# Start of a one-layer decoder kernel: small weights in three loads, K's first quarter moved up, zero products, a set order for TensorE

## The chip, the cores and the metric

The kernel runs on one core of one Trainium2 chip. The metric is device time in microseconds (us) of one execution, the median over repeated runs. Engines are named as the profile does: PE (TensorE) does the matrix products, PEld is its weight load, ACT is ScalarE, DVE is VectorE, POOL is GpSimd, SP is SyncE, which here issues nearly all loads.

## What is computed

One layer of a hybrid decoder, batch 1, 512 positions, model width 1024, all float32. Cut to what matters here:

```python
def reference(x, norm_mix_g, w_in, conv_a_w, gdn_conv_w, gdn_A_log, gdn_dt_bias, gdn_norm_g,
              w_a_out, w_b_out, w_o, norm_ffn_g, w_up, ffn_conv_w, w_down, norm_final_g):
    h = rmsnorm(x, norm_mix_g)
    bg, cg, xv, q, k, v, z, a, b, ga, gb = split(h @ w_in)      # a and b are 8 wide, the others 1024
    y_a = (bg * causal_dwconv(cg * xv, conv_a_w)) @ w_a_out
    y_b = gdn_branch(q, k, v, z, a, b, gdn_conv_w, gdn_A_log, gdn_dt_bias, gdn_norm_g) @ w_b_out
    x = x + (sigmoid(ga) * y_a + sigmoid(gb) * y_b) @ w_o
    h = rmsnorm(x, norm_ffn_g)
    x = x + conv_ffn(h, w_up, ffn_conv_w, w_down)               # D_FF = 2816
    return rmsnorm(x, norm_final_g)
```

The change touches only the beginning: the first `rmsnorm`, the turned activations, and the first products with `w_in` (those of `k`, and of `a` and `b`).

## The kernel before

**Products in two parts.** Every large product is made of three products of a one-pass type (fp32r): a float32 operand is split into a rounded part (`wh`, `hT[0]`) and the rest (`wl`, `hT[1]`), and high times high, high times low and low times high are added up in PSUM. The rounded part is made by ACT, the rest by DVE. Weights come as *blocks* of 1 MB, 256 output columns each; a block has four quarters (256 KB), and each quarter is split by one ACT copy and one DVE subtraction (`Block.part`, L135 to L141). A list of *jobs* (block, use) is worked through by `run_jobs`; the split of the next block is fed in while the products of the current one are issued. Block 0 is K, columns 0 to 255; block 1 is Q.

**The beginning, stage by stage.** `x` comes in four tiles `xt` of 128 positions (512 KB; the first two in halves). For a tile t: `norm_x(t)` squares and sums (ACT, L480), turns the sum into a factor (DVE L485 and L482, then a power on POOL, L486); `scale_x(t)` multiplies (DVE, L491); `turn_x(t)` transposes the tile on PE in eight pieces of 128 columns k = 0 to 7 (L496). Tiles 0 and 1 are the first half of the positions, 2 and 3 the second. For each half and each k, `out_hi` makes `hT[0]` (ACT, L499) and `out_lo` makes `hT[1]` (DVE, L503), both with the norm's weight from the tile `wA`.

K's block is treated by hand: its quarters are loaded one by one (`load_k`, L379) and split by `round_k(q)` (ACT, L509) and `rest_k(q)` (DVE, L513). `k_tile(j, k)` issues three products for output column group j on the first half of the positions; `ab_tile(k)` two products for `a` and `b`. All of them go through `mm`, so the profile shows them at L108.

**Small weights.** Convolution weights, norm weights and the gates' biases are small. Before, `wr` (128 rows of 128, from three loads, L446 to L448) is transposed on PE and copied by DVE into `wA` (L535); `wr2` and `wr3` (three loads, L463 to L466) are transposed later and copied into `wF` (L573 to L575); `dtb` and `alg` are two loads that broadcast eight numbers to all partitions (L458, L460); `ab_raw` is one load (L450).

**What sets the order.** SP issues loads in program order. Between L528 and L571 the order on DVE, ACT and POOL is the written one (`manual_schedule`); the order on PE, and all that follows on every engine, is set at build time by a planner with its own estimates of when operands are ready. `tc.keep_in_program_order` pins an instruction behind the one that was written before it on its engine. A few products of zeros (`WARM`, L470) run on PE while the first loads are under way.

The order as it is written for the first half of the positions:

```python
            for ks in (lower, upper):
                for k in ks:
                    out_hi(0, bs, k)
                for k in ks:
                    out_lo(0, bs, k)
                    k_tile(0, k)
                    ab_tile(k)
                if ks is lower:
                    rest_k(1)
```

After it come `norm_x(2)`, `rest_k(3)`, `scale_x(2)`, `norm_x(3)`, `rest_k(2)`, `scale_x(3)`, then `k_tile(1, k)` for the lower four k, `turn_x(2)` and `turn_x(3)`, `k_tile(1, k)` for the upper four, and `out_hi` and `out_lo` of the second half.

## Time and profile before

| | |
|---|---|
| time, median of 3 runs | 966.83 us (965.64 to 966.93) |
| profiled execution | 966.41 us, of which the span is 964.7 us |
| busy in the span | PE 99%, DVE 77%, ACT 52%, POOL 16% |
| part that the change touches | from the start to about 31 us, where the products of block 1 begin |

The span is the time from the first to the last instruction of the program; the 1.7 us beside it lie outside the program. A row of the timeline gives start and duration in us, engine, line, operation, output and inputs, shapes and count, and in brackets how long the engine had stood idle before it and what ended that. A row of a table of stretches gives busy time and instructions of each engine, then the TensorE clock that was granted (1.00 is full), the busy share of the DMA engines and what they moved.

### The profile page before, as it was taken

What the parts mean: (1) busy time and instruction counts of PE and PEld (TensorE: products, weight loads), DVE (VectorE), ACT (ScalarE), POOL (GpSimd) and SP (SyncE); (2) the same over time, 40 slices, a digit from 0 to 9 for tenths busy, and PEclk for the clock granted to TensorE, in tenths of its full rate; (3) what the DMA queues carried; (4) which work ended last, traced back from release to release, by engine and by line L of the source; (5) the groups of instructions that cost most, each with busy time, mean ns of one, the idle gap of its engine ahead of it and who ended that gap; (6) DMA issues with size and microseconds to landing.
All of it is one profiled execution on the core that took longest, in us unless ns stands there. A gap on an engine that the chain in (4) does not pass through costs nothing.

```text
span 964.7 us, 16169 instructions
## 1 busy us (share of the span) xinstructions
PE 951.5 (99%) x6178; PEld 822.6 (85%) x6178; DVE 743.1 (77%) x1401; ACT 505.9 (52%) x1073; POOL 157.1 (16%) x251
## 2 busy tenths in 40 slices
PE   8999999999999999999999999999999999999996
PEld 6888887887878889999988888998889999888885
DVE  5968686796735957799863479999988888969775
ACT  6795656566444424444751235645645456546463
POOL 3330300202000202312232100223222210000000
PEclk9999999999999999999999999999999999999999
DMA  6443422213121456756878436594774783176332
GB/s 227 155 139 95 121 53 89 74 47 103 53 88 45 133 130 138 200 147 160 232 256 173 124 104 225 149 232 154 174 189 177 193 163 131 45 260 230 99 131 87
DMA packets 51630, 138.11 MB, mean 143 GB/s; under 512 B 21692, under 2 KB 22113, under 8 KB 42849
## 3 DMA queue, kind: packets, MB, share of 16 engines
q1 hardware_dynamic: 38864, 107.45, 32.5%
q0 software_dynamic: 12544, 29.37, 16.3%
q8 instruction: 48, 0.79, 0.3%
q14 instruction: 30, 0.24, 0.1%
q10 hardware_dynamic: 144, 0.26, 0.1%
HBM read 133.64 MB, written 32.78 MB: 173 GB/s over the span
## 4 chain that ended last, share of the span: by engine, by line
PE 91%; DVE 4%; ACT 1%; issue 1%; POOL 1%; POOLq 0%
PE ps L108 83%; PE ps L681 1%; PE ps L716 1%; DVE wl L141 1%; PE ps L890 1%; PE ps L910 1%; DVE h L1327 1%; PE ps L899 0%; DVE hn L1313 0%; PE ps L878 0%; PE ps L877 0%; PE ps L854 0%; PE ps L848 0%; POOL r L1311 0%; PE ps L792 0%
## 5 line engine op out<-in xcount | busy, mean ns | idle before, releaser
L108 PE MATMUL ps<-hT,wh 128*128 128x512 f32 (+1 forms) x1104 | 319.1, 368 | 1.6 <-ACT hT L499 1.5
L140 ACT CAST wh<-raw 128x512 fp32r<-128x512 f32 x350 | 203.0, 618 | 220.8 <-PE ps L108 142.5
L141 DVE TENSOR_TENSOR wl<-raw,wh 128x512 fp32r<-128x512 f32 x350 | 232.3, 689 | 58.5 <-ACT wh L140 57.5
L108 PEld LDWEIGHTS ps<-hT,wh 128*128 128x128 f32 x1104 | 197.4, 190 | 30.6 <-ACT hT L499 1.7
L108 PE MATMUL ps<-hT,wl 128*128 128x512 f32 (+1 forms) x552 | 195.4, 362 | 0.0
L108 PE MATMUL ps<-h,wh 128*128 128x512 f32 (+1 forms) x704 | 177.7, 341 | 0.4 <-DVE h L1327 0.4
L108 PEld LDWEIGHTS ps<-h,wh 128*128 128x128 f32 x704 | 122.3, 189 | 15.7 <-DVE h L1327 0.6
L108 PEld LDWEIGHTS ps<-hT,wl 128*128 128x128 f32 x552 | 104.6, 190 | 13.8
L108 PE MATMUL ps<-h,wl 128*128 128x512 f32 (+1 forms) x352 | 114.5, 341 | 0.0
L108 PE MATMUL ps<-wh,xs 128*128 128x512 f32 (+1 forms) x320 | 96.9, 384 | 0.0
L108 PEld LDWEIGHTS ps<-h,wl 128*128 128x128 f32 x352 | 66.6, 189 | 7.6
L108 PEld LDWEIGHTS ps<-wh,xs 128*128 128x128 f32 x320 | 59.6, 188 | 13.1
L223 POOL COPY gate<-raw 1x1 f32<-1x1 f32 x38 | 19.7, 518 | 272.9 <-DMA raw<-in_w_in_dram 119.7
L108 PE MATMUL ps<-wl,xs 128*128 128x512 f32 (+1 forms) x160 | 62.1, 388 | 0.0
L108 PE MATMUL ps<-ts,wh 128*128 128x256 f32 x320 | 56.2, 276 | 0.0
L338 DVE SCALAR_TENSOR_TENSOR cv<-ps,wA,cv 128x511 f32<-128x511 f32 (+2 forms) x72 | 53.2, 741 | 3.9 <-ACT cv L335 3.7
L140 ACT CAST wh<-raws 128x512 fp32r<-128x512 f32 x66 | 39.2, 618 | 26.9 <-PE ps L108 8.6
L141 DVE TENSOR_TENSOR wl<-raws,wh 128x512 fp32r<-128x512 f32 x66 | 42.9, 687 | 12.6 <-ACT wh L140 12.5
L161 DVE TENSOR_TENSOR raw<-raw 128x512 f32<-128x512 f32 x72 | 49.4, 686 | 1.4
L108 PEld LDWEIGHTS ps<-ts,wh 128*128 128x128 f32 x320 | 49.0, 188 | 0.0
L108 PE MATMUL ps<-us,wh 128*128 128x256 f32 x256 | 45.0, 276 | 0.0
L108 PE MATMUL ps<-yas,wh 128*128 128x512 f32 x128 | 40.3, 394 | 0.0
(316 smaller groups left out, 1546.2 us busy)
## 6 DMA issues: line engine op xcount, KB each, us to landing
raw<-in_w_in_dram SPq DMA_DIRECT2D x35, 1024.0 KB, 4.9
raw<-in_w_up_dram SPq DMA_DIRECT2D x22, 1024.0 KB, 5.0
dv<-in_w_down_dram POOLq DMA_DIRECT2D x50, 256.0 KB, 6.2
raws<-dv SPq DMA_DIRECT2D x8, 768.0 KB, 7.2
ov<-in_w_o_dram POOLq DMA_DIRECT2D x20, 256.0 KB, 5.1
raws<-in_w_down_dram SPq DMA_DIRECT2D x10, 512.0 KB, 5.0
raw<-in_w_a_out_dram SPq DMA_DIRECT2D x4, 1024.0 KB, 5.9
raw<-in_w_b_out_dram SPq DMA_DIRECT2D x4, 1024.0 KB, 8.0
```

Source lines behind the costliest of these rows:

```text
L108: pe.matmul(o, lhsT=a, rhs=b, start=start, stop=stop, skip_group_check=free)
L140: act.copy(out=wh, in_=src)
L141: dve.tensor_tensor(out=wl, in0=src, in1=wh.bitcast(F32), op=ALU.subtract)
L161: dve.tensor_tensor(out=r[q], in0=a, in1=b, op=op)
L223: tc.keep_in_program_order(pool.tensor_copy(out=gate[:, 0:1], in_=el[:, 0:1]))
L338: dve.scalar_tensor_tensor(out=dst[:, sh:], in0=src[:, :S - sh], scalar=wcol(j), in1=dst[:, sh:], op0=ALU.mult, op1=ALU.add)
L681: pe.transpose(out=o[:, n * P:(n + 1) * P], in_=src[:, n * P:(n + 1) * P], identity=ident)
L716: pe.matmul(o[:, i], lhsT=kqs[:, a, h, 0, sl], rhs=kqs[:, b, h, :, sl], start=a > 0, stop=a + b == 0)
L890: pe.matmul(o[:, 0:P], lhsT=TTf[:, f, :], rhs=rs[h], start=True, stop=True)
L910: pe.matmul(o[:, 0:P], lhsT=A[:, f, :], rhs=vns[h], start=True, stop=True)
L1327: dve.tensor_tensor(out=h2[1][:, 4 * g:4 * g + 4, t * P:(t + 1) * P], in0=ov, in1=hs.bitcast(F32), op=ALU.subtract)
```

## The change

- SP's loads: `load_k(0)` becomes the fifth load, right behind the four loads of `x`'s first half. The small weights come in three loads that the host has laid out: `small_mix` (128 x 128, straight into `wA`), `small_ab`, and `small_rest` (128 x 149: `wF`, `dtb` and `alg` side by side) as the last one. There are 13 loads instead of 19, and PE's three transposes of small weights and DVE's two copies of them are gone.
- PE gets three products of zeros of 128 columns behind `turn_x(0)` and two behind `turn_x(1)` (`busy`), in float32 like `WARM`.
- PE's order is now the written one too, up to L571. In it, four k at a time: for each k, high times high, high times low and the two products for `a` and `b`; then the four products with `wl`.
- DVE's `rest_k(0)` is moved from ahead of the first `out_lo` to behind the second one; `rest_k(1)` likewise to behind the second `out_lo` of the upper four.
- The split of block 1 (Q) is pinned in program order on ACT and DVE (`pinned`).

```diff
             wl = self.wl[name] = wp.tile([P, *self.quarter], F32R, tag="wl", bufs=WQ, name=nm("wl"))
-            act.copy(out=wh, in_=src)
-            dve.tensor_tensor(out=wl, in0=src, in1=wh.bitcast(F32), op=ALU.subtract)
+            ops = act.copy(out=wh, in_=src), dve.tensor_tensor(out=wl, in0=src, in1=wh.bitcast(F32), op=ALU.subtract)
+            if self.pinned:
+                for op in ops:
+                    tc.keep_in_program_order(op)
...
+    rest_w = const.tile([P, 133 + 2 * H], F32, name="rest_w")
+    wF = rest_w[:, 0:133]
+    dtb, alg = rest_w[:, 133:133 + H], rest_w[:, 133 + H:133 + 2 * H]
...
         load_x(0)
         load_x(1)
-        wr = st1.tile([P, P], F32, name="wr")
-        nc.sync.dma_start(out=wr[0:96], in_=gdn_conv_w.rearrange("o j (c p) -> (o j c) p", p=P))
-        nc.sync.dma_start(out=wr[96:120], in_=conv_a_w.rearrange("o j (c p) -> (o j c) p", p=P))
-        nc.sync.dma_start(out=wr[120:128], in_=norm_mix_g.rearrange("o (c p) -> (o c) p", p=P))
+        load_k(0)
+        nc.sync.dma_start(out=wA, in_=small_mix)
         ab_raw = st1.tile([P, ND, 16], F32, name="ab_raw")
-        nc.sync.dma_start(out=ab_raw, in_=w_ab)
-        load_k(0)
+        nc.sync.dma_start(out=ab_raw, in_=small_ab)
         load_k(1)
         load_x(2)
         load_x(3)
         load_k(3)
         load_k(2)
-        dtb = gs.tile([P, H], F32, name="dtb")
...
-        nc.sync.dma_start(out=wr3[66:67], in_=gdn_norm_g)
+        nc.sync.dma_start(out=rest_w, in_=small_rest)
...
+        def busy(n, cols):
+            for _ in range(n):
+                pe.matmul(po[:, 0:cols], lhsT=warm[:, 0:P], rhs=warm[:, 0:cols], start=True, stop=True)
+
+        busy(WARM, S)
...
+        def first_tiles(ks, q):
+            for i, k in enumerate(ks):
+                out_lo(0, bs, k)
+                if i == 1:
+                    rest_k(q)
+                for e in (0, 1):
+                    mm(o_k[0][:, 0:HS], piece(k_block.wh, 0, k), hT[e][:, k, 0:HS], k == 0 and e == 0, False)
+                ab_tile(k)
+            for k in ks:
+                mm(o_k[0][:, 0:HS], piece(k_block.wl, 0, k), hT[0][:, k, 0:HS], False, k == ND - 1)
...
-        with tc.manual_schedule(engines={mybir.EngineType.DVE, mybir.EngineType.Activation, mybir.EngineType.Pool}):
+        with tc.manual_schedule(engines={mybir.EngineType.DVE, mybir.EngineType.Activation, mybir.EngineType.Pool,
+                                         mybir.EngineType.PE}):
             norm_x(0)
             scale_x(0)
             turn_x(0, bs)
-            pe.transpose(out=po[:, 0:P], in_=wr, identity=ident)
+            busy(3, P)
             norm_x(1)
             round_k(0)
-            dve.tensor_copy(out=wA, in_=po[:, 0:P])
             scale_x(1)
             turn_x(1, bs)
+            busy(2, P)
             ab_split()
             round_k(1)
-            rest_k(0)
             o_ab, o_k = bank(), [bank(), bank()]
-            for ks in (lower, upper):
+            for q, ks in enumerate((lower, upper)):
                 for k in ks:
                     out_hi(0, bs, k)
-                for k in ks:
-                    out_lo(0, bs, k)
-                    k_tile(0, k)
-                    ab_tile(k)
-                if ks is lower:
-                    rest_k(1)
+                first_tiles(ks, q)
             norm_x(2)
...
-        po = bank()
-        pe.transpose(out=po[:, 0:66], in_=wr2, identity=ident[:66, :66])
-        pe.transpose(out=po[:, 66:133], in_=wr3, identity=ident[:67, :67])
-        dve.tensor_copy(out=wF, in_=po[:, 0:133])
...
     jobs.insert(14, jobs.pop(11))
+    jobs[1][0].pinned = True
```

## The prediction

> **What bounds the kernel now.** First the page: busy shares and the chain of work that ended last.

> ```profile
> PE 951.5 (99%) x6178; PEld 822.6 (85%) x6178; DVE 743.1 (77%) x1401; ACT 505.9 (52%) x1073; POOL 157.1 (16%) x251
> PE 91%; DVE 4%; ACT 1%; issue 1%; POOL 1%; POOLq 0%
> ```

> TensorE is the bound throughout, so a change at the start is worth what it brings forward the moment from which PE is never idle again. Second, PE's waits: in the first 45 us (four rows), and from there to the end (two rows); us, times, longest.

> ```profile
> PE ps L496 <- DVE xr L491: 1.6, 2, 1.2
> PE ps L470 <- DVE warm L431: 1.5, 1, 1.5
> PE ps L108 <- ACT hT L499: 1.5, 1, 1.5
> PE ps L108 <- DVE hT L503: 0.2, 1, 0.2
> ...
> PE ps L681 <- DVE vs L929: 0.5, 1, 0.5
> PE ps L108 <- DVE h L1327: 0.4, 1, 0.4
> ```

> All there is to gain from waits lies ahead of the products. Third, a table of stretches, cut where the granted clock (the fraction after POOL) changes.

> ```profile
> 4.86:8.27 3.41, 2.35 (x12) 1.16 (x10) 1.62 (x7) 1.52 (x6) 1.10 (x2) 1.00 0.76 245
> 8.27:11.69 3.42, 1.45 (x11) 1.21 (x11) 1.76 (x5) 2.12 (x6) 0.00 (x0) 1.00 0.86 304
> 11.69:15.10 3.41, 3.25 (x16) 2.74 (x15) 3.41 (x9) 3.41 (x9) 0.00 (x0) 0.50 0.70 230
> 15.10:19.28 4.18, 4.18 (x37) 4.10 (x36) 3.23 (x8) 1.84 (x4) 2.63 (x4) 1.00 0.70 237
> 30.00:40.00 10.00, 10.00 (x51) 8.46 (x51) 9.63 (x19) 7.15 (x12) 7.58 (x19) 1.00 0.48 188
> ```

> The clock is halved for 3.41 us, right behind a stretch of that length in which PE was busy 1.45 us; 2.35 us in the stretch ahead did not halve it. A product of 256 columns takes 3.41/16 = 0.213 us while it is halved, 4.18/37 = 0.113 us afterwards. Fourth, the timeline of each engine, quoted where it is used.

> **The change part by part.**

> *Loads.* SP issues one after the other:

> ```profile
> 0.80 1.81 SPq L440 DMA_DIRECT2D xt<-in_x_dram  x4
> 2.65 0.43 SPq L446 DMA_DIRECT2D wr<-in_gdn_conv_w_dram  x1
> 3.13 0.44 SPq L447 DMA_DIRECT2D wr<-in_conv_a_w_dram  x1
> 3.61 0.27 SPq L448 DMA_DIRECT2D wr<-in_norm_mix_g_dram  x1
> 3.92 0.36 SPq L450 DMA_DIRECT2D ab_raw<-in_w_ab_dram  x1
> 4.32 0.90 SPq L379 DMA_DIRECT2D raw<-in_w_in_dram  x2
> ...
> xt<-in_x_dram SPq DMA_DIRECT2D x4, 256.0 KB, 4.5
> raw<-in_w_in_dram SPq DMA_DIRECT2D x4, 256.0 KB, 7.0
> ```

> K's first quarter moves from 4.32 to 2.65. The second stood at 4.32 + 0.45 = 4.77; now it follows the first (0.45), one load of small weights (0.44) and `ab_raw` (0.36): 3.90, that is 0.87 earlier. What ACT does with them:

> ```profile
> 9.57 0.62 ACT L509 CAST wh<-raw 128x512 fp32r<-128x512 f32 x1 [2.19 <-DMA raw<-in_w_in_dram]
> 10.10 0.29 ACT L391 CAST ab<-ab_raw 128x128 fp32r<-128x128 f32 x1
> 10.29 0.61 ACT L509 CAST wh<-raw 128x512 fp32r<-128x512 f32 x1
> 10.81 3.02 ACT L499 ACTIVATE hT<-ps,wA 128x256 fp32r<-128x256 f32 x8
> ...
> 20.69 3.03 ACT L499 ACTIVATE hT<-ps,wA 128x256 fp32r<-128x256 f32 x8 [3.75 <-PE ps L496]
> 23.56 2.22 ACT L140 CAST wh<-raw 128x512 fp32r<-128x512 f32 x4
> ```

> The first quarter took 9.57 - 4.32 = 5.25 us, so it lands near 7.90. The second is written ahead of `out_hi`, so it becomes the gate: it was there by 10.29 (no wait is shown), and with the same transit it is there by 9.42. Bounds: transit as the four quarters have it (7.0) puts it at 10.90; as x's halves have it (4.5), at 8.40. I take 9.42, the row of this very load; `out_hi` follows 0.52 later (10.81 - 10.29), at 9.94 instead of 10.81. `small_mix` is issued before that quarter, so it hides under it; the later loads, `small_rest` and Q's among them, are issued six loads earlier and are hidden by work that ends after 20 us.

> *DVE.*

> ```profile
> 10.63 0.68 DVE L513 TENSOR_TENSOR wl<-raw,wh 128x512 fp32r<-128x512 f32 x1
> 11.68 1.66 DVE L503 SCALAR_TENSOR_TENSOR hT<-ps,wA,hT 128x256 fp32r<-128x256 f32 x4 [0.36 <-ACT hT L499]
> 13.25 0.68 DVE L513 TENSOR_TENSOR wl<-raw,wh 128x512 fp32r<-128x512 f32 x1
> 13.85 1.65 DVE L503 SCALAR_TENSOR_TENSOR hT<-ps,wA,hT 128x256 fp32r<-128x256 f32 x4
> 18.46 0.75 DVE L491 TENSOR_SCALAR xr<-xt,rt 128x1024 f32<-128x1024 f32 x1 [0.44 <-POOL rt L486]
> ```

> `out_lo` begins 0.87 behind `out_hi` (11.68 - 10.81): at 10.81. From its start to the last one's end were 15.50 - 11.68 = 3.82 us with one `rest_k` inside; the second now costs 0.60 (13.85 - 13.25) in the chain instead of filling the wait ahead of it. So 10.81 + 4.42 = 15.23, against 15.50: of the 0.87 only 0.27 is left for DVE. Behind it are queued `rest_k(3)`, `scale_x(2)`, `rest_k(2)` and `scale_x(3)`; PE waits for the last of these. It ended at 19.21 and will at 18.94. The copy into `wA` is gone, but stood in an idle stretch: nothing.

> *TensorE.*

> ```profile
> 8.78 1.09 PE L496 MATMUL ps<-ident,xr 128*128 128x128 f32 x8 [1.15 <-DVE xr L491]
> 11.33 0.38 PE L108 MATMUL ps<-hT,wh 128*128 128x256 f32 x1 [1.46 <-ACT hT L499]
> 19.40 1.91 PE L496 MATMUL ps<-ident,xr 128*128 128x128 f32 x16
> 22.46 0.28 PE L108 MATMUL ps<-hT,wh 128*128 128x256 f32 x1
> 22.58 0.22 PE L573 MATMUL ps<-ident,wr 66*128 66x66 f32 x1
> 22.67 2.09 PE L108 MATMUL ps<-hT,ab 128*32 128x256 f32 x14
> 31.36 0.40 PE L108 MATMUL ps<-hT,wl 128*128 128x512 f32 x1
> ```

> Zero products: the row nearest in shape is the transpose, 1.91/16 = 0.12 us. Each product in float32 is two instructions (`WARM`'s three show as six), so `busy(3)` is 0.7 us and `busy(2)` 0.5, both in idle time: bounds 0 and 0.5, of which I take 0, since PE is free from 9.87 and the first product comes at 9.94 + 0.52 = 10.46.

> The set order makes PE wait for each `out_lo` in turn, where it could take other ready products before; queued behind such a wait are the products of the next k, which need a later `out_lo` anyway, and the `wl` products, of which four fill the 0.60 of each `rest_k`. So this costs nothing while DVE is the bound; without that cover a wait would cost at most one `out_lo` of 0.4.

> Does the clock stay? In 8.27 to 11.69, PE will have the transposes (1.09), `busy(2)` (0.47), one product at 10.46 (0.2), and from the first `out_lo`'s end (10.81 + 1.66/4 = 11.23) 0.46: 2.2 us. That is near the 2.35 that kept the clock and far from the 1.45 that lost it. I take it as kept, at some 7 in 10.

> With it, the products of the first half end 7 x 0.113 = 0.8 behind the last `out_lo` (the last k's three and four with `wl`): 16.0. `k_tile(1)` for four k (12 x 0.113 = 1.36) ends at 17.4, `turn_x(2)` (8 x 0.12) at 18.3. Then PE waits 0.7 for `scale_x(3)`: what was PE's bound becomes DVE's. `turn_x(3)` starts at 19.0; before, as the ninth of sixteen, at 19.40 + 8 x 0.12 = 20.35. Gain 1.35. All behind it (12 products, `out_hi`, `out_lo`, `use_ab`) is the same work in the same distances, and PE was the bound there; the two transposes of small weights cost 22.67 - 22.58 = 0.09. Sum 1.44 us at the first product of block 1: 31.36 becomes 29.9.

> *The pinned split.* Q's split stood behind `hT` before (23.56, after 20.69 + 3.03), so for its first quarters nothing changes. The last quarter now stands behind the gates' last exponential on ACT, written before it:

> ```profile
> 30.19 0.23 ACT L621 ACTIVATE t<-t 128x32 f32<-128x32 f32 x1 [0.84 <-DVE t L620]
> ```

> 30.42 - 1.44 + 0.62 + 0.68 = 30.3; it is read by Q's second half only, 24 products of 10.00/51 = 0.2 us behind 29.9, at 34.6. Covered by 4.3 us; without that cover each us late is a us.

> The profiled execution took 966.41 (span 964.7 and 1.7 around it), 0.42 below the median of the three runs. 966.41 - 1.44 = 964.97; from the median it would be 965.4. I predict 965.1.

> **The rivals.**

> *The clock is halved all the same.* Then (15.10 - 11.23)/0.213 = 18 products and the first one are done by 15.10, and 21 of the 40 remain (2.37): 17.5, 18.8 with `k_tile(1)`, 19.8 with `turn_x(2)`: gain 20.35 - 19.8 + 0.09 = 0.6: 965.8. Against it: 2.2 against 1.45. For it: no row lies between 1.45 and 2.35. The three runs spread by 1.3 us, which a stretch that falls otherwise would explain. [...]

> *The loads are bound by bytes, not by issuing.* Ahead of K's second quarter stand the same bytes as before. In 8.27 to 11.69 the DMA engines were busy 0.86; in 4.86 to 8.27 only 0.76, which speaks for room. If it lands at 10.29 as before, `out_hi` stays at 10.81, the last `out_lo` ends at 10.81 + 0.87 + 4.42 = 16.1, which is 0.6 later than before, and `scale_x(3)` with it: `turn_x(3)` starts at 19.9, gain 0.57 with the clock kept. But PE's stretch then holds only 1.09 + 0.47 + 0.2 = 1.8 us, so the clock may go as well: 15 products by 15.10, 25 behind them (2.83), and 20.25 for `turn_x(3)`: gain 0.2. Some 966.2. [...]

> *Slower: K's second quarter comes late.* One place, ACT's cast ahead of `out_hi`, in which everything of the first half is queued. Landing at 10.90, `out_hi` starts at 11.42 and the first `out_lo` ends at 12.7; with the clock halved 12 products are done by 15.10 and 28 remain (3.16), so PE reaches `turn_x(3)` at 18.3 + 1.36 + 0.96 = 20.6, and with the 0.09 it is 0.16 slower: 966.6. Beyond that each us late is a us; slower by 0.2% from about 12.7. Against it: it is issued earlier, with no more ahead of it.

> *The gain is given back.* DVE is busy 9.63 of 10 us from 30 to 40. If it bounds there, PE's 1.44 is lost: 966.4. Against it: DVE's own chain comes forward as well, and PE shows no wait there. What the planner places otherwise behind the start is unknown and can cost as well.

> **How the numbers follow.** Forecast 0.57 (of it 0.12 with the quarter at 8.4 to 8.9, down to 964.1); clock halved 0.14; bytes 0.13; given back 0.09; late, or worse placing, 0.07. The range reaches from 963.9 (quarter at 8.40 and a little scatter) to 967.1 (late end plus half of the runs' spread). 0.2% is 1.9 us, about what a measurement of this kernel tells from no change, and the forecast lies below it: faster takes the early landings and half as much again from the runs' scatter, 0.24; slower 0.07; within 0.69.

> **What would show it.** Right: first cast of K near 7.9, second near 9.4, `hT` from 9.9; granted clock 1.00 from 4.9 on; last `out_lo` ending near 15.2; a PE wait of about 0.7 for `xr` ahead of `turn_x(3)` at 19.0; first product of 512 columns near 29.9. Wrong: a second cast with a long DMA wait, a stretch at 0.50, PE waits behind 30 us, or other orders of groups later on.

## The result, and the profile after

The changed kernel took 971.5 us (median of 6 runs, 970.45 to 972.95) against 966.31 of the kernel before (6 runs, 964.71 to 966.93): a ratio of 1.0061, 95% interval 1.005 to 1.0071, so it is slower by 0.6%. 965.1 had been forecast. The profiled execution took 972.95 (span 971.2).

First the page of the changed kernel, the row of busy times. PE, 99% busy as before, is busy 8.2 us longer than the 951.5 of before, with 7 instructions more:

```profile
PE 959.7 (99%) x6185; PEld 829.3 (85%) x6185; DVE 744.4 (77%) x1399; ACT 507.2 (52%) x1073; POOL 158.8 (16%) x251
```

Second, PE's waits (us in total, times, longest), first 45 us and then the rest:

```profile
PE ps L107 <- ACT hT L495: 1.9, 1, 1.9
PE ps L465 <- DVE warm L435: 1.5, 1, 1.5
PE ps L107 <- DVE hT L499: 0.5, 1, 0.5
...
PE ps L680 <- DVE vs L928: 0.5, 1, 0.5
PE ps L107 <- DVE h L1327: 0.2, 1, 0.2
```

The waits for `xr` (1.6 before) are gone, the one for `hT` grew from 1.5 to 1.9, and behind the start there is nothing new. So whatever is lost later is lost while PE works. Third, the start in stretches (us, PE busy, PEld, DVE, ACT, POOL, granted clock, DMA share, GB/s); the last row is the halved stretch, the one above it the 3.41 us ahead of that:

```profile
8.27:11.69 3.42, 1.62 (x13) 1.35 (x12) 0.74 (x3) 1.26 (x4) 0.00 (x0) 1.00 1.00 370
9.89:13.30 3.41, 1.06 (x7) 0.81 (x7) 1.18 (x3) 2.57 (x7) 0.00 (x0) 1.00 1.06 420
13.30:16.71 3.41, 3.41 (x17) 3.05 (x17) 3.41 (x10) 3.41 (x8) 0.02 (x1) 0.50 0.45 189
```

The clock was halved again, from 13.30 (11.69 before), and the 3.41 us ahead of it held 1.06 us of PE work (1.45 before). The timeline of the start:

```profile
2.65 0.43 SPq L383 DMA_DIRECT2D raw<-in_w_in_dram  x1
...
4.07 0.43 SPq L383 DMA_DIRECT2D raw<-in_w_in_dram  x1
...
7.09 0.62 ACT L505 CAST wh<-raw 128x512 fp32r<-128x512 f32 x1
...
10.73 0.62 ACT L505 CAST wh<-raw 128x512 fp32r<-128x512 f32 x1 [1.69 <-DMA raw<-in_w_in_dram]
11.26 3.02 ACT L495 ACTIVATE hT<-ps,wA 128x256 fp32r<-128x256 f32 x8
12.12 0.87 DVE L499 SCALAR_TENSOR_TENSOR hT<-ps,wA,hT 128x256 fp32r<-128x256 f32 x2 [2.75 <-ACT hT L495]
12.91 0.68 DVE L509 TENSOR_TENSOR wl<-raw,wh 128x512 fp32r<-128x512 f32 x1
13.51 1.65 DVE L499 SCALAR_TENSOR_TENSOR hT<-ps,wA,hT 128x256 fp32r<-128x256 f32 x4
...
20.43 1.91 PE L492 MATMUL ps<-ident,xr 128*128 128x128 f32 x16
...
32.28 0.40 PE L107 MATMUL ps<-hT,wl 128*128 128x512 f32 x1
```

K's first quarter is in place at 7.09 (before: waited for until 9.57), but ACT then waits 1.69 us for the second, and `out_hi` starts at 11.26, 0.45 later than before. The first transpose of `turn_x` for the second half follows at 20.43 (19.40 before), and the first product of 512 columns at 32.28 (31.36 before, 29.9 in the forecast). So the start lost 1.03 us at the one and 0.92 us at the other, where 1.44 was to be gained. Nearly all else is lost far behind it. The answers for single tiles give, for each group of products, the duration (ns: least, median, most) and the start of the first and the last (us). Before:

```profile
L108 PE MATMUL ps<-ts,wh x320: 276/276/286, 358.1 to 473.1; 128*128 128x256 f32 x160
L108 PE MATMUL ps<-yas,wh x128: 394/394/394, 486.9 to 531.5; 128*128 128x512 f32 x128
L108 PE MATMUL ps<-us,wh x256: 276/276/286, 664.3 to 814.3; 128*128 128x256 f32 x128
L108 PE MATMUL ps<-wh,xs x320: 276/388/392, 849.9 to 957.0; 128*128 128x512 f32 x152, 128*128 128x256 f32 x8
```

After:

```profile
L107 PE MATMUL ps<-ts,wh x320: 279/281/285, 358.8 to 476.3; 128*128 128x256 f32 x160
L107 PE MATMUL ps<-yas,wh x128: 392/398/398, 490.2 to 534.7; 128*128 128x512 f32 x128
L107 PE MATMUL ps<-us,wh x256: 279/281/285, 667.7 to 819.7; 128*128 128x256 f32 x128
L107 PE MATMUL ps<-wh,xs x320: 277/393/404, 855.4 to 964.1; 128*128 128x512 f32 x152, 128*128 128x256 f32 x8
```

The stage of `ts` takes 117.5 us instead of 115.0, that of `us` 152.0 instead of 150.0, that of `xs` 108.7 instead of 107.1: 6.1 us, same instructions, no wait. A product of `ts` and `wh` follows the last after 118.8 ns on the mean, where it was 113.6; one of `wh` and `xs` after 232.3 instead of 227.5.

What the change did there stands in one line of its diff: `rest_w` is 149 columns wide where `wF` had 133. The pool in which it lies comes first in SBUF; all that is placed on that side behind it (`hT`, `yb`, the rings of `raw`, `wh` and `wl`) starts 64 bytes further. What lies on the other side (`ts`, `us`, `yas`, `mix`, `xs`) stays. In the compiled layouts `wh` begins 32 bytes behind a multiple of 256 before and 96 behind it after; `ts`, `us`, `yas` and `xs` 224 behind it in both. (No view here prints these layouts; the table of pairs below is their test.) Exactly the groups whose two operands lie on different sides changed their rate; those of `hT` or `h` with `wh`, which moved together, kept theirs (median duration 389 ns in both kernels). For `yas` it evens out: its products with `wh` became slower (median duration 394, then 398), those with `wl` faster (394, then 392), and the stage keeps its 44.6 us (44.5).

### The profile page after: what moved, and what is told of

Its sections match the earlier page's. It is cut to its first block, busy times and chain, and to the rows that moved or that the text cites. A ratio compares the mean times of both kernels' runs of the same rounds, so it can differ in the third digit from the quotient of the medians.

```text
span 971.2 us, 16169 instructions
## 1 busy us (share of the span) xinstructions
PE 959.7 (99%) x6185; PEld 829.3 (85%) x6185; DVE 744.4 (77%) x1399; ACT 507.2 (52%) x1073; POOL 158.8 (16%) x251
## 4 chain that ended last, share of the span: by engine, by line
PE 92%; DVE 4%; ACT 1%; issue 1%; DMA 1%; POOL 1%; SPq 0%; POOLq 0%
PE ps L107 84%; PE ps L680 1%; PE ps L715 1%; DVE wl L139 1%; DMA raw<-in_w_in_dram 1%; PE ps L889 1%; PE ps L909 1%; DVE h L1327 0%; PE ps L898 0%; DVE hn L1313 0%; PE ps L877 0%; PE ps L876 0%; PE ps L853 0%; PE ps L847 0%; POOL r L1311 0%
## 5 line engine op out<-in xcount | busy, mean ns | idle before, releaser
L139 DVE TENSOR_TENSOR wl<-raw,wh 128x512 fp32r<-128x512 f32 x350 | 232.3, 688 | 61.0 <-ACT wh L139 60.0
L107 PE MATMUL ps<-ts,wh 128*128 128x256 f32 x320 | 58.6, 282 | 0.0
## 6 DMA issues: line engine op xcount, KB each, us to landing
dv<-in_w_down_dram POOLq DMA_DIRECT2D x50, 256.0 KB, 6.2
ov<-in_w_o_dram POOLq DMA_DIRECT2D x20, 256.0 KB, 5.1
```

Of the source, the lines that this page charges most:

```text
L107: pe.matmul(o, lhsT=a, rhs=b, start=start, stop=stop, skip_group_check=free)
L139: ops = act.copy(out=wh, in_=src), dve.tensor_tensor(out=wl, in0=src, in1=wh.bitcast(F32), op=ALU.subtract)
```

## The experiments

In the runs' records stands each execution's mean granted clock. A halved stretch of 3.41 us lowers it by 3.41 x 0.5/965 = 0.0018, and that shows: of 63 executions of the kernel before beside these experiments, 24 had 0.998 or more (median 965.02) and 39 had 0.996 or 0.997 (966.3). A halved start costs some 1.3 us, and it happens in most executions, not in all. Where a per cent's tenth matters, times are compared "at full clock" (0.998 or more).

### The place: four runs

e1_before_moved64: the kernel before, with the 64 bytes moved in front.

```diff
-    wF = const.tile([P, 133], F32, name="wF")
+    wF = const.tile([P, 133 + 2 * H], F32, name="wF")
...
-        dtb = gs.tile([P, H], F32, name="dtb")
+        dtb = wF[:, 133:133 + H]
...
-        alg = gs.tile([P, H], F32, name="alg")
+        alg = wF[:, 133 + H:133 + 2 * H]
```

> The kernel before, instruction for instruction; only the two 8-column tiles dtb and alg lie behind wF in its pool instead of in the pool gs, so that everything placed between them (hT, yb, the rings wh and wl, the raw weights) starts 64 bytes further, as it does in the changed kernel. Theory 1 (place): the 6 us that the changed kernel loses behind its start come from these addresses alone, product by product: products of ts and wh at 118.8 ns instead of 113.6, of xs and wh at 232.3 instead of 227.5, no wait more, about 972 us (970.5 to 973). Theory 2 (order): they come from the other order that the planner gives DVE and ACT: this order is untouched, 966.3 us. Theory 3 (start): they follow from the later start of the second block: also 966.3 us.

Measured: 971.44 us (5 runs) against 966.1, ratio 1.0061 (1.0048 to 1.0073): the whole loss of the changed kernel, with none of its edits to loads, order or engines. Its tiles show the rates of the changed kernel:

```profile
L108 PE MATMUL ps<-ts,wh x320: 279/281/285, 356.8 to 474.3; 128*128 128x256 f32 x160
L108 PE MATMUL ps<-us,wh x256: 279/281/285, 665.8 to 817.8; 128*128 128x256 f32 x128
L108 PE MATMUL ps<-wh,xs x320: 277/393/404, 853.4 to 962.2; 128*128 128x512 f32 x152, 128*128 128x256 f32 x8
```

117.5, 152.0 and 108.8 us, to a tenth those of the changed kernel. Order and start fall as causes of these 6 us.

e2_after_back64: the changed kernel with the old addresses.

```diff
-    rest_w = const.tile([P, 133 + 2 * H], F32, name="rest_w")
+    rest_w = const.tile([P, 133], F32, name="rest_w")
...
+        heads = gs.tile([P, 2 * H], F32, name="heads")
+        nc.sync.dma_start(out=heads, in_=small_heads)
```

> The changed kernel with every tile back at the address it has in the kernel before: the heads' 16 columns leave rest_w for a tile of their own in gs, with a load of their own at the end of SP's queue (one DMA more, wanted only by gates_chain). Place: only the start's loss is left, 1.0 us at the second half's first turn_x and about 0.7 later, 966.3 + 0.7 = 967.0 us (966.0 to 968.0), products of ts and wh at 113.6 ns. Order and start: still 971 to 972 us, products at 118.8.

Measured: 964.84 us (11 runs) against 966.1, ratio 0.9993 (0.9984 to 1.0002). The place accounts for what was lost behind the start. At full clock it is 964.60 against 965.21 of the kernel before beside it, where some 0.7 more had been expected: the start's later `turn_x` costs nothing that is seen at the end. How it is made up for was not followed; with the clock kept in both profiles, the first product of block 1 starts at 30.73 here and at 29.59 in e1, the first one of `ts` at 357.3 and 356.8. Of the 11 executions 9 are at full clock.

e3_after_more64: the same tiles another 64 bytes on (`mask16` moved in front too; `wh` 160 behind a multiple of 256).

> As the run before, but mask16 (32 columns) moved from gs to the pool in front, so the same tiles lie 128 bytes behind their place in the kernel before, 64 behind that in the changed kernel. If the place counts by its remainder by 128 bytes: as with the addresses of before, 967.0 us (966 to 968), products of ts and wh at 113.6 ns. If any move away from the old place costs (absolute place, a bank boundary): 971 us or more. Order and start: 971 to 972.

Measured: 971.17 us (4 runs), ratio 1.0056 (1.0041 to 1.0071). The remainder by 128 is the same as before, and it is as slow as with 64: the remainder by 128 is not what counts.

e4_address_table: the pairs by themselves, in one execution. Stationary tiles `sa` to `sh` lie 128, 160, 192, 224, 0, 32, 64, 96 bytes behind a multiple of 256, moving tiles `ma` to `mh` likewise.

> Not the layer: 128 groups of 16 back-to-back float32r products on copies of x, each group with one of 8 stationary tiles and one of 8 moving tiles, which lie 0, 32, ... 224 bytes behind a multiple of 256; first 256 moving columns, then 512; the output is x. Place: the time from one product's start to the next depends on the pair of remainders: near 113.7 ns for 256 columns where they differ by 64 (moving 96, stationary 32 by 128), 118 to 120 where they are equal; for 512 columns 227 to 228 against 232 to 233, in some pairs. Order and start: one value for all pairs, within 1 ns.

Two pieces of its timeline (start, length, 16 products a row), 512 columns on `se` and 256 columns on `sg`:

```profile
269.22 3.89 PE L59 MATMUL bank<-md,se 128*128 128x512 f32 x16
272.95 3.81 PE L59 MATMUL bank<-me,se 128*128 128x512 f32 x16
276.60 3.90 PE L59 MATMUL bank<-mf,se 128*128 128x512 f32 x16
280.34 3.83 PE L59 MATMUL bank<-mg,se 128*128 128x512 f32 x16
284.01 3.90 PE L59 MATMUL bank<-mh,se 128*128 128x512 f32 x16
...
116.61 1.98 PE L59 MATMUL bank<-me,sg 128*128 128x256 f32 x16
118.42 2.05 PE L59 MATMUL bank<-mf,sg 128*128 128x256 f32 x16
120.31 2.08 PE L59 MATMUL bank<-mg,sg 128*128 128x256 f32 x16
122.22 2.05 PE L59 MATMUL bank<-mh,sg 128*128 128x256 f32 x16
```

A row's start taken from the next one's, over 16, is the time per product. 512 columns: `me` on `se`, the same remainder, 228 ns; `mg`, 64 further, 229; `md`, `mf`, 233 to 234. 256 columns: `me` on `sg`, the moving slice 64 lower, 113; `mg`, the same remainder, 119. Over all 64 pairs of 512 columns it goes by the difference of the two remainders by 256: 0 gives 227 to 228, 64 gives 229 to 230, all others 232 to 234. For 256 columns (63 pairs, since the first cannot be told from the warm-up) seven of the eight pairs with the moving slice 64 lower lie at 113.6 to 115.5 and the eighth (192 and 128) at 117.8, all other pairs at 116.7 to 119.9; so there the difference is not the whole rule.

Read back into the layer (moving less stationary, by 256): `ts` on `wh` 224 - 32 = 192, that is 64 lower, before; 128 after; 64 in e3: 113.6, 118.8, 117.9 ns. `wh` on `xs` 64, 128 and 192: 227.5, 232.3, 233.5; the 227.5 is below the table's 229 to 230, but the products of `wl` between them take 231.7 there, 228.9 on the mean of all. `yas` on `wh`, 512 columns, 192, 128 and 64: the stage takes 44.6, 44.5 and 43.7 us, as the table has it (192 and 128 alike, 64 faster). The kernel before had the good difference in its two long stages.

### Which neighbour slows a product

e10_own_or_next: pairs of slices that alternate, in one execution.

> Not the layer: groups of 32 back-to-back products on copies of x whose stationary and moving slices alternate between two remainders by 256 bytes, so that a product's moving slice stands in one relation to its own stationary slice and in another to the next one's; the output is x. Four groups of 512 columns: both relations 0; own 0 and next 32 apart; own 32 apart and next 0; both 32. Four of 256 columns: both 192; own 192, next another; own another, next 192; both 128. Theory N (a product is slowed while the next product's weights are read): the second group at 233 ns, the third at 228; of 256 columns the second at 118 to 119, the third at 114. Theory O (it is the product's own weights): the other way round. Both count: all mixed groups between.

The first rows of the groups:

```profile
33.94 0.40 PE L61 MATMUL bank<-mc,sc 128*128 128x512 f32 x1
...
41.37 0.39 PE L61 MATMUL bank<-me,se 128*128 128x512 f32 x1
...
48.73 0.40 PE L61 MATMUL bank<-mg,sg 128*128 128x512 f32 x1
...
56.20 0.28 PE L61 MATMUL bank<-ma,sa 128*128 128x256 f32 x1
...
59.97 0.28 PE L61 MATMUL bank<-mc,sc 128*128 128x256 f32 x1
```

32 products each: 7.43/32 = 232 ns with the own weights at difference 0 and the next ones 32 away, 7.36/32 = 230 the other way round, 7.47/32 = 233 with both away; with both at 0, a product follows the last after 227. So both relations count, and neither alone decides. Here the next product's weights, whose load starts with this product in the trace of the kernel before (the product of `ts` and `wh` and the next one's load, both at 358.07), weigh more than its own (5 to 6 ns against 3). For 256 columns it tells nothing: the group that should be fast took 3.77/32 = 118, since it was built on the eighth pair of the table.

### The start: five runs, all with the old addresses

e5_rest_ahead: `rest_k(0)` back in front of `out_hi`.

```diff
             round_k(1)
+            rest_k(0)
...
-                if i == 1:
+                if q and i == 1:
                     rest_k(q)
```

> The changed kernel with the old addresses (e2_after_back64) and one edit: rest_k(0) goes back in front of the first out_hi, where DVE waits for ACT anyway; rest_k(1) stays behind out_lo(5). In e2's trace, with the clock at full speed, the first product starts at 11.15 and the first transpose of turn_x(2) at 18.65, 7.50 later; in e1's trace (order of before, clock at full speed) 10.50 and 17.27, 6.77 later. Theory A (DVE's chain): the 0.68 us of rest_k(0) between out_lo(1) and out_lo(2) is what PE waits for, so turn_x(2) starts 6.8 to 6.9 behind the first product, near 18.0, and executions at a granted clock of 0.998 and more fall from e2's 964.6 to 964.0. Theory B (PE's order): PE has its work set anyway; 18.6 and 964.6.

Measured: 966.3 us (10 runs), ratio 1.0 (0.999 to 1.0009); 3 executions at full clock, median 964.57, and 7 below, 966.54. In its profile the chain of `out_lo` is 3.83 us long (11.79 to 15.62), 4.42 in e2: the 0.60 was in the chain. In time it brings nothing that is seen (964.57 against 964.60), but three executions from 963.63 to 965.61 cannot tell theory A's 964.0 from theory B's 964.6, so that stays open. That the clock was lost more often than in e2 was not expected by either.

e6_round_later: also `round_k(1)` behind the lower `out_hi`.

```diff
-            round_k(1)
             rest_k(0)
...
                     out_hi(0, bs, k)
+                if not q:
+                    round_k(1)
```

> As e5_rest_ahead, and round_k(1) goes behind the lower four out_hi, so that ACT no longer waits for K's second quarter (10.11 in e2, 10.73 in the changed kernel) before the first out_hi. Theory A (the wait for that transfer is the start's loss): first out_hi at 9.3 to 9.6, first product at 10.3 (behind the two zero products, which end at 10.29 in e2), turn_x(2) near 17.2, executions at full clock near 963.3. Theory B (the transfer is late anyway): the upper half's products wait for the cast instead, PE shows an idle time before its fifth tile of 0.5 us or more, turn_x(2) stays near 18.0 and the time at 964.0.

```profile
9.53 1.57 ACT L497 ACTIVATE hT<-ps,wA 128x256 fp32r<-128x256 f32 x4 [0.31 <-PE ps L494]
...
10.97 0.63 ACT L507 CAST wh<-raw 128x512 fp32r<-128x512 f32 x1
11.47 1.59 ACT L497 ACTIVATE hT<-ps,wA 128x256 fp32r<-128x256 f32 x4
```

Measured: 963.63 us (11 runs), ratio 0.9978 (0.9969 to 0.9987); 10 executions at full clock, 963.61. `out_hi` starts at 9.53, the first product at 10.35, `turn_x` of the second half at 17.14 (18.65 in e2): theory A in all three, and 1.0 us of the 1.5 is kept to the end. The second quarter had arrived when its cast came.

e7_zeros_moved: `busy(3, P)` becomes `busy(4, P)`, `busy(2, P)` goes.

> As e6_round_later, with four zero products behind turn_x(0) instead of three and none behind turn_x(1), where the first product can now follow at once. Theory A (idle stretches of PE close the clock): no stretch is left over 0.5 us between the first transpose and the first product, so every execution keeps the clock (0.998 and more; 9 of 11 did in e2), first product near 9.9, about 0.2 us less than e6, 963.1. Theory B (the clock hangs on how long PE has been at work before, or on nothing that this kernel sets): one execution in two to one in five still at 0.996 or 0.997, about 1.2 us longer than the others.

Measured: 963.62 us (11 runs), ratio 0.9976 (0.9967 to 0.9985), all 11 at full clock; first product at 10.02. The 0.2 us more did not come.

e8_before_zeros: the kernel before with `busy(3, P)` behind the transpose of `wr`, `busy(2, P)` behind `turn_x(1)`, and PE in the set order.

> The kernel before with one part of the change alone: three zero products of 128 columns behind the transpose of wr, two behind turn_x(1), and PE's order set in this stretch. Nothing of it lies on the path (PE idles there until the first out_hi). Theory A (zero products keep the clock): nearly all executions at 0.998 and more, where 7 of 15 of the kernel before were, and a median near 965.1 against 966.1 us. Theory B (they do not): the same share of about one in two, the same 966.1 us.

Measured: 965.09 us (11 runs), ratio 0.9993 (0.9984 to 1.0002); 9 of 11 at full clock, median there 965.09 against 965.08 without. Of the kernel before beside it 11 of 33 were. Theory A: the zero products, with the set order, save no work; they save the clock, in more of the executions. The two were not taken apart.

e11_k1_ahead: in e2, the load of K's second quarter directly behind the first.

```diff
         load_k(0)
+        load_k(1)
         nc.sync.dma_start(out=wA, in_=small_mix)
...
-        load_k(1)
```

> e2_after_back64 with one edit: K's second quarter is issued right behind the first (at 3.12 instead of 4.09), ahead of small_mix and small_ab. Theory A (it lands after its issue in its turn): the second cast starts about 1.0 earlier, near 9.1 to 9.4 instead of 10.1 to 10.9, first out_hi near 9.9 and executions at full clock at 964.0, against 964.6. Theory B (x2 and x3, issued right behind, take their share of the same engines, and only the bytes issued up to then count): it lands at 10.0 or later as before, 964.6 us; or small_mix becomes what the first out_hi waits for.

```profile
9.10 0.30 ACT L394 CAST ab<-ab_raw 128x128 fp32r<-128x128 f32 x1 [1.05 <-DMA ab_raw<-in_small_ab_dram]
9.30 0.62 ACT L507 CAST wh<-raw 128x512 fp32r<-128x512 f32 x1
9.82 3.02 ACT L497 ACTIVATE hT<-ps,wA 128x256 fp32r<-128x256 f32 x8
```

Measured: 964.55 us (11 runs), ratio 0.9988 (0.9979 to 0.9997), all at full clock. Issued two loads earlier, the quarter was there by 9.30, without a wait: theory A for the landing, 0.8 us at the first `out_hi`. In the profiles the 0.8 reaches the first product of block 1 (29.92, 30.73 in e2) and the span (962.5, 963.3). The medians at full clock do not show it (964.55, 964.60), but the kernel before had 964.84 and 965.21 at full clock beside them; what it is worth stays open.

The share of executions at full clock, put together: with PE idle for 0.3 us or less ahead of the first product (e6, e7, e8, e9, e11) 45 of 49; with zero products, but an idle stretch of 0.9 to 1.9 us there (changed kernel, e2, e3, e5) 19 of 31, from 3 of 10 (e5) to 9 of 11 (e2); without zero products (the kernel before) 24 of 63. The next run's kernel, whose clock is lost elsewhere, is left out of this.

The traces show what lies behind the shares. In each the changes of the clock stand on a grid of 3.41 us (in the profile of before the clock is halved at 11.69 and again at 960.60, behind PE's last product: 948.91 us, 278 times 3.413), and the grid begins at another moment in each execution: the halved stretch starts at 11.69 there, at 12.29 in e5 and at 13.30 in the changed kernel, none a whole number of 3.41 us from another. By this grid, a stretch with 0.58 us of PE work (e12), 1.06 (changed kernel), 1.45 (before) or 1.59 (e5) was followed by a halved one, and one with 1.87 (e3), 2.04 (e2), 2.15 (e12, and the changed kernel from 962.21) or more by full clock; only a stretch at the end of e1 (960.88 to 964.30) lies across, with 1.56 and full clock behind it. Two of these rows, e5's and e3's:

```profile
8.88:12.29 3.41, 1.59 (x12) 1.20 (x10) 1.30 (x4) 1.89 (x5) 0.00 (x0) 1.00 1.02 393
...
7.81:11.22 3.41, 1.87 (x15) 1.49 (x14) 1.08 (x3) 1.50 (x4) 0.38 (x1) 1.00 0.99 375
```

So what counts in these traces is PE's work in such a stretch, near 1.6 of 3.41 us, and the same gaps can fall into one stretch in one execution and into two in the next.

### The pinned split

e12_not_pinned: e7 without `jobs[1][0].pinned = True`.

> e7_zeros_moved without the line that pins the second block's split behind hT; the planner places these eight operations. The prediction costed the pinning at nothing: 963.6 us, within 0.3. Rival: pinned, the casts delay something of the next block; without it 963.0 or less, or with it the weights come in time that would be late without it, 964.2 or more.

Measured: 970.29 us (4 runs), ratio 1.0048 (1.0034 to 1.0062), 6.7 us more than e7: the last rival, and far beyond its 964.2. PE's waits from 20 to 70 us, and two stretches (columns as above, the clock behind POOL):

```profile
PE ps L107 <- DVE kn L704: 3.4, 1, 3.4
PE ps L659 <- DVE G L649: 1.6, 1, 1.6
```

```profile
62.00:64.00 2.00, 2.00 (x6) 1.63 (x7) 2.00 (x5) 1.95 (x9) 1.16 (x1) 0.64 0.00 0
64.00:66.00 2.00, 2.00 (x6) 1.52 (x6) 2.00 (x9) 1.47 (x8) 0.52 (x1) 0.51 0.00 0
```

e7 has no wait there. 5.0 us of waits and, behind the long one, the clock halved for 3.4 us (2 x 0.36 + 2 x 0.49 = 1.7) make 6.7 of the 7.2 us between the two profiled executions (971.12 and 963.91); that the medians differ by 6.7 too is chance, for two of the four executions are at full clock and still take 969.06 and 969.46. Left free, the chain of `G` and `kn` comes late: DVE makes `G` at 46.53 and the second `kn` at 61.22, in e7 at 43.43 and 53.24. In the kernel before, with nothing pinned, they come at 45.81 and 55.87, and PE does not wait. That it is the planner's order of ACT and DVE alone was not tested.

### A version that beats both

e9_row_operands_moved: e7 with `yas`, `mix`, `mixb` and `xs` put at difference 0 to `wh`.

```diff
+    def slot(pool, tag, name, shape, off):
+        t = pool.tile([P, ND * S + 64], F32R, tag=tag, name=name)[:, off:off + ND * S]
...
-        st["ts"] = [sc.tile([P, 4, 4, HS], F32R, tag=f"t{i}", name=f"ts{i}") for i in range(2)]
+        st["ts"] = [slot(sc, f"t{i}", f"ts{i}", (4, 4, HS), 0) for i in range(2)]
...
-        st["yas"] = [st["sc"].tile([P, ND, S], F32R, tag=f"t{i}", name=f"yas{i}") for i in range(2)]
+        st["yas"] = [slot(st["sc"], f"t{i}", f"yas{i}", (ND, S), 16) for i in range(2)]
```

> e7_zeros_moved, with the operands yas, mix, mixb and xs 64 bytes behind the start of their slots (slots 256 bytes larger, so that ts and us keep their remainders): the moving operand of these products then lies at the same remainder by 256 bytes as the stationary one (difference 0, where it is 192 for yas and 64 for the others). Place, by the table of pairs (difference 0: 227 to 228 ns for 512 columns, 192: 233, 64: 229 to 230): products of yas fall from 233.3 to 227 to 228 (192 of them, -1.1 us), those of wl and xs from 231.7 (152, -0.6 us), those of wh and xs stay at 227.5; 963.6 - 1.7 = 961.9 us (961.4 to 962.6). If the place explains only what the 64 bytes of this change did: 963.6, rates as before.

```profile
L107 PE MATMUL ps<-ts,wh x320: 276/276/286, 356.0 to 471.0; 128*128 128x256 f32 x160
L107 PE MATMUL ps<-yas,wh x128: 389/389/389, 484.9 to 528.1; 128*128 128x512 f32 x128
L107 PE MATMUL ps<-wh,xs x320: 278/389/389, 846.2 to 952.3; 128*128 128x512 f32 x152, 128*128 128x256 f32 x8
```

Measured: 961.41 us (5 runs), ratio to the kernel before 0.9954 (0.9942 to 0.9966), 2.2 us less than e7. The stage of `yas` takes 43.2 us, 44.6 in the kernel before; that of `xs` 106.1, 107.1 before; `ts` stays at 115.0. The per-product means are 226.5 to 227.0 ns for these groups (233.3 for `yas`, 231.7 for `wl` and `xs` before). It is 10 us less than the changed kernel, with the same products but for one zero product fewer.

## Why the prediction was wrong, step by step

- *"A change at the start is worth what it brings forward the moment from which PE is never idle again"*, and with it the sum 966.41 - 1.44 = 964.97. This is the step that failed: it carries the gain at block 1 to the end, and so takes every product behind it at the rate of before. They are the same products at other rates: with no new wait, `ts`, `us` and `xs` took 6.1 us more. Some 6 us come from 64 bytes (e1: +5.3 in the median, +6.1 at full clock). The prediction's sentence on "the same work in the same distances" held for the part that it names: from the first transpose of `turn_x(2)` to the first product of 512 columns it is 11.85 us, 11.96 before. With the addresses put back (e2) the kernel takes 964.84, which is the forecast of 965.1, but by luck: the second quarter is cast at 10.11, `out_hi` starts at 10.63 and the first product of 512 columns at 30.73, none of them as forecast. "What the planner places otherwise" was weighed at 0.07 together with late loads; it was not the planner either, but where tiles lie, which no part of the prediction looked at.
- *K's first quarter near 7.9*: there by 7.09. *The second at 9.42, between 8.40 and 10.90*: 10.73, 6.66 us behind its issue at 4.07, where 5.52 behind 3.90 had been taken (the loads follow each other after 0.47 to 0.48, the sum had taken 0.36 to 0.45). The mechanism (it becomes the gate) was right, the transit was mis-sized; the DMA share from 8.27 to 11.69 was 1.00, where the row of before with 0.86 had been read as room. By e11 its place among the loads counts: there by 9.30 when issued two loads earlier, 10.11 to 10.73 in three traces with the place of the change (e2, e5, changed kernel). The nearest was the rival "Slower: K's second quarter comes late", with 10.90 and `out_hi` at 11.42. Hence `out_hi` at 11.26 instead of 9.94.
- *`out_lo`'s chain of 4.42 behind its start*: 12.12 to 16.55. That term held.
- *The clock kept, 7 in 10, by 2.2 us of PE work in the stretch*: 1.62 us from 8.27 to 11.69, because the first product came late. But that stretch was laid where the grid of before had it; in this execution the stretch ahead of the halved one is 9.89 to 13.30, with 1.06 us. 4 of the 6 executions kept the clock. The direction was right (e8: 9 of 11 at full clock, 11 of 33 of the kernel before beside it), and so was the measure, PE's work in 3.41 us; what it lacked is that the grid moves from execution to execution. The same kernel falls now on one side and now on the other: 24 of 63 executions of the kernel before were at full clock, and the halved stretch starts at 11.69, 12.29 and 13.30 us in three profiles (before, e5, changed kernel). The prediction read one profiled execution as the kernel's rule.
- *Gain 1.44 at the first product of block 1*: -0.92 in the profiles (32.28 against 31.36), both with a halved stretch. What the forecast had in mind is what e6 brings, once ACT does not wait for the second quarter: `turn_x` at 17.14.
- *The set order of PE costs nothing*: not separated from the zero products, but e8 has both and is at full clock as fast as without (965.09, 965.08).
- *The pinned split costs nothing*: nothing speaks against it; without it e7 loses 6.7 us, which no step foresaw.

## What to carry to other kernels

When a small tile grows, look at what moves behind it: if PE is the bound, compare the same group of products in both profiles, first start to last start and median duration, before looking for a wait. Operands that are streamed and loaded together should lie at a chosen distance by 256 bytes (here, in e4, 0 for 512 columns of float32r, 227 to 228 ns against 229 to 234, and the moving slice 64 lower for 256, in seven of eight pairs 113.6 to 115.5 ns against 116.7 to 119.9), and that distance is best set by the layout and not left to the sum of what comes first in the pool. A clock that is halved in one profile may be kept in the next run (of the kernel before 24 of 63 executions were at full clock, 39 not): read the granted clock of every run before pricing it.
